# A two-layer diffusion step on one core: the first MLP's modulation sums and residual adds move from GpSimd and ScalarE to VectorE

## Chip, cores and metric

The kernel runs on one core of a Trainium2 chip. The metric is the device time of one launch in microseconds (us), the median of several runs. Engines: PE is TensorE (matrix products; its weight loads are listed as PEld), DVE is VectorE, ACT is ScalarE, POOL is GpSimd. SP only issues DMAs, in the order of its queue.

## The reference, cut to what matters

Two layers (one of differential attention, one of neighbourhood attention), each followed by a dense MLP, over 640 tokens (512 latent, 128 context) of width 1024. Every sub-layer has shift, scale and gate vectors that come from a conditioning vector. There are two conditions, `c` for the latent tokens and `c_ctx` for the context tokens, so each of the six vectors of a layer exists twice.

```python
def modulation(cond, w_ada_l, b_ada_l):
    m = (jax.nn.silu(cond) @ w_ada_l + b_ada_l)[:, None, :]
    return jnp.split(m, 6, axis=-1)

def mlp_residual(x, shift, scale, gate, g, w1, w2):
    h = rms_norm(x, g) * (1 + scale) + shift
    return x + gate * (jnp.square(jax.nn.relu(h @ w1)) @ w2)

for l in range(DEPTH):
    mp = modulation(cond_ctx, w_ada[l], b_ada[l])
    ms = modulation(c, w_ada[l], b_ada[l])
    ...
    yp = mlp_residual(yp, mp[3], mp[4], mp[5], norm_mlp_g[l], w_fc1[l], w_fc2[l])
    ys = mlp_residual(ys, ms[3], ms[4], ms[5], norm_mlp_g[l], w_fc1[l], w_fc2[l])
```

## The kernel before

All products are split into float32r parts: every operand is a high part (a ScalarE copy, L55) and a low part (a subtraction, L56, on VectorE here), and each product is three matmuls (hi·hi, hi·lo, lo·hi).

**The first MLP** runs from 473 to 932 us of the span, in four quarters q of 1024 hidden columns. In each, `fc1` loads three blocks of weights, makes eight column tiles `pz` of 48 matmuls each (L1076), and turns each into a tile `u`: ReLU and square on ScalarE, then the two parts. `fc2` then takes three blocks of columns (384, 256 and 384 wide) times five token tiles, in pairs (0, 1), (2, 3) and (4), 24 matmuls each (L160). `add_gated` closes each: VectorE multiplies the PSUM by the gate into `tmp` (L984), and then `tmp` is added to `x` (L985), on GpSimd in the first MLP and on VectorE in the second. The last block of q = 3 is a function of its own (`last_chunk`), with the add on VectorE already.

In the first block of a quarter the last two of the eight steps over the hidden columns are left to the end, for tile 0 and then for tile 1. In the built order PE's rest of tile 1 stands behind a wait for tile 0's `tmp`, since both lie in one PSUM tile. So VectorE's queue at that place can stop PE. I call it the boundary of a quarter.

**Beside it** `ada_fma` computes 14 half vectors of modulation without PE: the gate of layer 0's MLP and all six vectors of layer 1. A half vector (a job) is eight units: a DMA brings 128 rows of 512 columns (`fraw`, 256 KB, a ring of five buffers), and for both conditions the rows times a scalar per partition are added to `acc`. Condition 0 is one VectorE instruction (L439). Condition 1 is a ScalarE product into `ftmp` (two buffers, L441) and a GpSimd addition (L442). The first unit of a job writes instead of adding (L436 on VectorE, L437 on ScalarE). A finished job is summed over the partitions by PE: with eight transposes (L406) and a VectorE sum (L407) for shift and scale, with eight products by ones (L417) and a VectorE add (L418) for a gate. A gate goes to DRAM (L421); layer 0's is read back to all partitions (L453) and is wanted by the first `tmp`. 24 units are taken over the first fc1, the rest over the quarters that follow.

**What sets the order**: in this stretch a scheduler orders each engine's instructions from its own estimate of their times. Every engine, and SP's queue, then runs its list in order, and an instruction that waits holds back all behind it.

Of the kernel before, what the change touches and what calls it, by code (L numbers as in the profile page):

```python
# [7 lines left out]
F32 = mybir.dt.float32  # L8
F32R = mybir.dt.float32r
AF = mybir.ActivationFunctionType  # L10
ALU = mybir.AluOpType
# [4 lines left out]
P = 128  # L16
# [29 lines left out]
class Kernel:  # L46
# [333 lines left out]
                    nc.sync.dma_start(self.gate_d[l, vec // 3, :, c0 : c0 + 256], row)  # L380
            yield

    def ada_fma(self, jobs, pool, ahead, gate=None, share=False, wait=()):

        nc = self.nc
        units = [(job, kt) for job in jobs for kt in range(KT)]  # L390
        raws = []

        def load():
            (l, vec, h), kt = units[len(raws)]
            raw = pool.tile([P, 512], F32, tag="fraw", bufs=ahead + 1, name="fraw")
            nc.sync.dma_start(raw, self.I["w_ada"][l, kt * P : (kt + 1) * P, vec * D + h * 512 : vec * D + h * 512 + 512])
            raws.append(raw)

        def finish(l, vec, h, acc):
            c0 = vec * D + h * 512  # L400
            if vec % 3 < 2:
                pv = self.small.tile([P, 4, 2], F32, tag="pv", bufs=2, name="pv")
                for ci in range(2):
                    pt = self.psum_t()
                    for k in range(4):
                        nc.tensor.transpose(pt[:, k], acc[:, ci, k * P : (k + 1) * P], self.ident)  # L406
                    nc.vector.tensor_reduce(pv[:, :, ci], pt, AX.X, ALU.add)  # L407
                self.cols_out(l, vec, h * 4, 4, pv)
                return

            pb = self.psum_g(256)
            row = pool.tile([P, 512], F32, tag="ftmp", bufs=2, name="row")[:, 0:256]
            for j in range(4):
                cs = slice(j % 2 * 256, j % 2 * 256 + 256)
                src = self.I["b_ada"][l : l + 1, c0 + cs.start : c0 + cs.stop]
                nc.sync.dma_start(row[32 * j : 32 * j + 32], src.partition_broadcast(32))
                nc.tensor.matmul(pb[32 * j : 32 * j + 32], self.ones[:, 0:32], acc[:, j // 2, cs], start=True, stop=True)  # L417
            nc.vector.tensor_tensor(row, pb, row, ALU.add)  # L418
            for j in range(4):
                dst = self.gate_d[l, vec // 3, j // 2 : j // 2 + 1, h * 512 + j % 2 * 256 : h * 512 + j % 2 * 256 + 256]  # L420
                nc.sync.dma_start(dst, row[32 * j : 32 * j + 1])  # L421
            if l == 0 and h == 1:
                self.load_gate(0, gate)

        for _ in range(ahead):
            load()
        yield
        done = None
        for i, (job, kt) in enumerate(units):
            if i + ahead < len(units):  # L430
                load()
            raw = raws[i]
            s = [self.silu[:, ci, kt : kt + 1] for ci in range(2)]
            if kt == 0:
                acc = pool.tile([P, 2, 512], F32, tag="acc", bufs=2, name="acc")
                nc.vector.tensor_scalar(acc[:, 0], raw, s[0], None, ALU.mult)  # L436
                nc.scalar.activation(acc[:, 1], raw, AF.Identity, scale=s[1])  # L437
            else:
                nc.vector.scalar_tensor_tensor(acc[:, 0], raw, s[0], acc[:, 0], ALU.mult, ALU.add)  # L439
                tmp = pool.tile([P, 512], F32, tag="ftmp", bufs=2, name="ftmp")  # L440
                nc.scalar.activation(tmp, raw, AF.Identity, scale=s[1])  # L441
                (nc.vector if share and kt % 3 == 2 else nc.gpsimd).tensor_tensor(acc[:, 1], acc[:, 1], tmp, ALU.add)  # L442
            if done and kt == dict(wait).get(i // KT, 4):
                finish(*done)
            if kt == KT - 1:
                done = (*job, acc)
            yield
        finish(*done)
        yield

# [657 lines left out]
    def fc2(self, l, q, us, gate, fill, chunks=CHUNKS):  # L1108
        act = lambda kt, t: (us[kt][:, 0, t * P : (t + 1) * P], us[kt][:, 1, t * P : (t + 1) * P])
        for c0, n in chunks:  # L1110
            ww = self.load_block(self.I["w_fc2"][l], q * D, c0, n)

            for ts in ((0, 1), (2, 3), (4,)):
                if len(ts) == 2:
                    pair = self.psum.tile([P, 2, 512], F32, tag="s", bufs=self.PS, name="ps_g")
                    ps = [pair[:, i, :n] for i in range(2)]
                else:
                    ps = [self.psum_g(n)]
                late = KT - 2 if c0 == 0 and ts[0] == 0 else KT
                for i, t in enumerate(ts):  # L1120
                    for _ in self.product_steps(ps[i], act, t, ww, 0, late, last=late == KT):
                        pass
                for i, t in enumerate(ts):
                    if late < KT:
                        for _ in self.product_steps(ps[i], act, t, ww, late, KT, first=False):
                            pass
                    self.add_gated(self.x[t], ps[i], gate, t, c0, n, c0, None if l else self.nc.gpsimd)
                    if l and q == 3:
                        self.store(t, c0, n)
                    fill.go(n / D / NT / 2)  # L1130
# [226 lines left out]
```

## Time and profile before

| | us |
|---|---|
| median of 3 runs (1768.11 to 1772.25) | 1770.71 |
| the profiled execution | 1769.35 |
| its span | 1767.6 |
| PE busy in the span | 1696.0 (96%) |
| DVE busy | 1059.5 (60%) |
| ACT busy | 881.7 (50%) |
| POOL busy | 591.5 (33%) |

Matmuls overlap each other and their weight loads, so PE's mean duration of one is longer than its share of the time; a count over a stretch gives the pace. [...] The second MLP has the same matmuls as the first, without the modulation beside it.

### The profile page before, as it was taken

The numbers are of one execution on the slowest core, as the hardware profiler recorded it, in microseconds if no ns is written. First come the engines' busy times: TensorE is split into PE (matmuls) and PEld (weight loads), VectorE is DVE, ScalarE is ACT, GpSimd is POOL, SyncE is SP. The second block draws the span as 40 slices with busy tenths as digits, with TensorE's granted clock in tenths as the row PEclk, the third lists the DMA queues.
The fourth block names the chain that finished last, engine by engine and source line by source line (L and its number), as shares of the span: only waits on it lengthen the run. The fifth ranks groups of instructions, "written<-read, shape, count | busy, mean of one in ns | idle before, by whom it ended". The sixth has DMA issues, their size and how long they took to land.

```text
span 1767.6 us, 30599 instructions
## 1 busy us (share of the span) xinstructions
PE 1696.0 (96%) x11365; PEld 1617.8 (92%) x11365; DVE 1059.5 (60%) x2148; ACT 881.7 (50%) x2491; POOL 591.5 (33%) x630
## 2 busy tenths in 40 slices
PE   7899999988998999989999999999989999999999
PEld 4689999978898999989998999998889999999999
DVE  5568888865797667456746666667572433424323
ACT  4466777753663453533526777777354232142230
POOL 1333444234566436435326644553350000000000
PEclk9899999999999999999999999999999999999999
DMA  9862355321355444434422433333132222222221
GB/s 301 238 190 68 77 132 154 93 90 37 121 178 167 131 143 137 145 108 128 135 85 65 124 81 100 97 102 90 46 120 60 87 73 69 85 71 73 71 92 51
DMA packets 210435, 195.11 MB, mean 110 GB/s; under 512 B 39446, under 2 KB 194126, under 8 KB 210286
## 3 DMA queue, kind: packets, MB, share of 16 engines
q1 hardware_dynamic: 210286, 193.16, 37.2%
q8 instruction: 89, 1.46, 0.4%
q14 instruction: 60, 0.49, 0.1%
HBM read 182.96 MB, written 16.45 MB: 113 GB/s over the span
## 4 chain that ended last, share of the span: by engine, by line
PE 77%; ACT 7%; DVE 6%; POOL 3%; issue 3%; DMA 3%; SPq 1%; DVEq 0%; POOLq 0%; ACTq 0%
PE ps_g L160 43%; PE pz L1076 21%; PE ps_t L724 2%; PE ps_t L898 2%; PE ps_t L753 1%; PE ps_s L748 1%; PE ps_s L747 1%; PE ps_t L887 1%; DVE acc L439 1%; POOL acc L442 1%; ACT E L797 1%; POOL rs L132 1%; ACT sq L643 1%; ACT rawh L650 1%; ACT hf L480 1%
## 5 line engine op out<-in xcount | busy, mean ns | idle before, releaser
L160 PE MATMUL ps_g<-w,hT 128*128 128x384 f32 (+1 forms) x2544 | 541.5, 348 | 11.3 <-DVE tmp L984 4.8
L160 PE MATMUL ps_g<-w,u 128*128 128x384 f32 (+1 forms) x2880 | 455.0, 319 | 13.9 <-DVE tmp L984 12.7
L160 PEld LDWEIGHTS ps_g<-w,u 128*128 128x128 f32 x2880 | 448.0, 189 | 17.8 <-DVE tmp L984 12.7
L1076 PE MATMUL pz<-hT,w 128*128 128x320 f32 x3072 | 457.9, 310 | 5.6 <-ACT hT L55 2.5
L1076 PEld LDWEIGHTS pz<-hT,w 128*128 128x128 f32 x3072 | 451.1, 188 | 9.4 <-ACT hT L55 3.6
L160 PEld LDWEIGHTS ps_g<-w,hT 128*128 128x128 f32 x2544 | 426.4, 192 | 24.3 <-ACT hT L55 6.3
L55 ACT ACTIVATE w<-raw 128x1152 fp32r<-128x1152 f32 (+1 forms) x162 | 150.2, 955 | 218.3 <-PE ps_g L160 204.9
L56 DVE TENSOR_TENSOR w<-raw,w 128x1152 fp32r<-128x1152 f32 (+1 forms) x150 | 183.0, 1243 | 103.8 <-ACT w L55 103.6
L984 DVE TENSOR_TENSOR tmp<-ps_g,gate 128x384 f32<-128x384 f32 (+1 forms) x170 | 82.8, 505 | 223.2 <-PE ps_g L160 219.8
L442 POOL TENSOR_TENSOR acc<-acc,ftmp 128x512 f32<-128x512 f32 x98 | 164.5, 1679 | 131.5 <-ACT acc L437 103.7
L132 POOL TENSOR_TENSOR rs<-var,mhalf 128x4 f32<-128x4 f32 (+1 forms) x120 | 103.0, 861 | 233.6 <-DVE var L131 231.3
L121 POOL TENSOR_TENSOR w<-raw,w 128x256 fp32r<-128x256 f32 x184 | 142.9, 796 | 85.7 <-ACT w L117 84.6
L985 POOL TENSOR_TENSOR x<-x,tmp 128x384 f32<-128x384 f32 (+1 forms) x95 | 94.0, 1002 | 165.7 <-DVE tmp L984 165.0
L56 DVE TENSOR_TENSOR u<-relu,u 128x640 fp32r<-128x640 f32 x64 | 63.6, 994 | 117.6 <-ACT u L55 117.5
L441 ACT ACTIVATE ftmp<-fraw,silu 128x512 f32<-128x512 f32 x98 | 70.8, 723 | 118.4 <-POOL acc L442 96.0
L1101 ACT ACTIVATE relu<-pz 128x640 f32<-128x640 f32 x64 | 44.7, 699 | 169.4 <-PE pz L1076 169.4
L439 DVE SCALAR_TENSOR_TENSOR acc<-fraw,silu,acc 128x512 f32<-128x512 f32 x98 | 127.3, 1299 | 2.7 <-DMA fraw<-in_w_ada 0.4
L650 ACT ACTIVATE rawh<-ps_g,rs 128x64 f32<-128x64 f32 x304 | 71.0, 325 | 40.4 <-POOL rs L132 40.4
L748 PE MATMUL ps_s<-kT,qT 128*128 128x320 f32 (+3 forms) x256 | 76.1, 302 | 0.0
L747 PE MATMUL ps_s<-kT,qT 128*128 128x320 f32 (+3 forms) x256 | 75.8, 307 | 0.2 <-ACT E L797 0.2
L643 ACT ACTIVATE sq<-ps_g 128x64 f32<-128x64 f32 x304 | 68.3, 225 | 7.2
L872 DVE CUSTOM_DVE_ANT_0 ps_s<-ps_s,bias 128x384 f32<-128x384 f32 x64 | 36.2, 566 | 43.8 <-PE ps_s L748 31.8
(183 smaller groups left out, 2066.2 us busy)
## 6 DMA issues: line engine op xcount, KB each, us to landing
raw<-in_w_fc SPq DMA_DIRECT2D x64, 576.0 KB
fraw<-in_w_ada SPq DMA_DIRECT2D x112, 256.0 KB
raw<-in_w_fc SPq DMA_DIRECT2D x64, 384.0 KB
raw<-in_w_qkv_diff SPq DMA_DIRECT2D x24, 512.0 KB
fraw<-in_w_ada SPq DMA_DIRECT2D x24, 512.0 KB
raw<-in_w_qkv_na SPq DMA_DIRECT2D x24, 512.0 KB
bias<-ball SPq DMA_DIRECT2D x64, 128.0 KB
araw<-in_w_ada SPq DMA_DIRECT2D x8, 768.0 KB
```

The costliest lines, as they stand in the source:

```text
L55: self.nc.scalar.activation(hi, src, AF.Copy)
L56: (eng or self.nc.vector).tensor_tensor(lo, src, hi.bitcast(F32), ALU.subtract)
L121: self.nc.gpsimd.tensor_tensor(lo[:, ks], raws[i][:, ks], hi[:, ks].bitcast(F32), ALU.subtract)
L132: nc.gpsimd.tensor_tensor(out, v[:, :n], self.mhalf[:, :n], ALU.pow)
L160: self.nc.tensor.matmul(ps, a, b, start=first and kt == k0 and i == 0, stop=last and kt == k1 - 1 and i == 2)
L439: nc.vector.scalar_tensor_tensor(acc[:, 0], raw, s[0], acc[:, 0], ALU.mult, ALU.add)
L442: (nc.vector if share and kt % 3 == 2 else nc.gpsimd).tensor_tensor(acc[:, 1], acc[:, 1], tmp, ALU.add)
L650: nc.scalar.activation(raw[:, u // 2, u % 2], ps[:, u * 64 : u * 64 + 64], AF.Identity, scale=rs[:, u : u + 1])
L747: self.nc.tensor.matmul(out, q[:, 0, u], k, start=True, stop=False)
L748: self.nc.tensor.matmul(out, q[:, 1, u], k, start=False, stop=True)
L985: (eng or nc.vector).tensor_tensor(x[:, c0 : c0 + n], x[:, c0 : c0 + n], tmp, ALU.add)
L1076: nc.tensor.matmul(pz[:, s, 0:HALF], wp[:, cs], self.hT[:, b, kt, s * HALF : (s + 1) * HALF], start=first and kt == 0, stop=last and kt == ...
```

## The change

For condition 1 the ScalarE product and the GpSimd addition are replaced by a second VectorE instruction of the form that condition 0 has. `add_gated` in `fc2` adds to `x` on VectorE in both layers. The gates' `row` gets a pair of buffers of its own, since the buffers that it shared with `ftmp` go.

```diff
-            row = pool.tile([P, 512], F32, tag="ftmp", bufs=2, name="row")[:, 0:256]
+            row = pool.tile([P, 256], F32, tag="frow", bufs=2, name="row")
...
                 nc.vector.tensor_scalar(acc[:, 0], raw, s[0], None, ALU.mult)
                 nc.scalar.activation(acc[:, 1], raw, AF.Identity, scale=s[1])
             else:
-                nc.vector.scalar_tensor_tensor(acc[:, 0], raw, s[0], acc[:, 0], ALU.mult, ALU.add)
-                tmp = pool.tile([P, 512], F32, tag="ftmp", bufs=2, name="ftmp")
-                nc.scalar.activation(tmp, raw, AF.Identity, scale=s[1])
-                (nc.vector if share and kt % 3 == 2 else nc.gpsimd).tensor_tensor(acc[:, 1], acc[:, 1], tmp, ALU.add)
+                for ci in range(2):
+                    nc.vector.scalar_tensor_tensor(acc[:, ci], raw, s[ci], acc[:, ci], ALU.mult, ALU.add)
...
-                    self.add_gated(self.x[t], ps[i], gate, t, c0, n, c0, None if l else self.nc.gpsimd)
+                    self.add_gated(self.x[t], ps[i], gate, t, c0, n, c0)
```

PE's order stays as it was, and so does the order of everything before and after the first MLP. On VectorE, ScalarE, GpSimd and SP the first MLP is ordered anew. Two places on VectorE follow. In the names, `u` and `w` are the low parts of hidden tiles and of weights, and `gate_6385` is the gate for the latent tokens.

VectorE ahead of the boundary of q = 0, from the add that closes the second half of layer 0's gate to the first `tmp`; before:

```order
L418 TENSOR_TENSOR row<-ps_g,row 128x256
L436 TENSOR_SCALAR acc<-fraw,silu 128x512
L439 SCALAR_TENSOR_TENSOR acc<-fraw,silu,acc 128x512 x2
L56 TENSOR_TENSOR w<-raw,w 128x3x256
L56 TENSOR_TENSOR u<-relu,u 128x640
L439 SCALAR_TENSOR_TENSOR acc<-fraw,silu,acc 128x512
L56 TENSOR_TENSOR w<-raw,w 128x3x256
L56 TENSOR_TENSOR w<-raw,w 128x2x256
L439 SCALAR_TENSOR_TENSOR acc<-fraw,silu,acc 128x512 x2
L984 TENSOR_TENSOR tmp<-ps_g,gate_6385 128x384
```

The same place of the changed kernel (its L440 is L439 of before, L982 and L983 are L984 and L985):

```order
L418 TENSOR_TENSOR row<-ps_g,row 128x256
L436 TENSOR_SCALAR acc<-fraw,silu 128x512
L440 SCALAR_TENSOR_TENSOR acc<-fraw,silu,acc 128x512 x4
L56 TENSOR_TENSOR u<-relu,u 128x640
L440 SCALAR_TENSOR_TENSOR acc<-fraw,silu,acc 128x512 x2
L56 TENSOR_TENSOR w<-raw,w 128x3x256 x2
L56 TENSOR_TENSOR w<-raw,w 128x2x256
L982 TENSOR_TENSOR tmp<-ps_g,gate_6385 128x384
L440 SCALAR_TENSOR_TENSOR acc<-fraw,silu,acc 128x512
L983 TENSOR_TENSOR x<-x,tmp 128x384
```

Six instead of five accumulations stand between the row and `tmp`, and the last `u` has four of them ahead of it. From the start of the MLP to this `tmp` there are 48 accumulations instead of 26.

VectorE ahead of the boundary of q = 2, from the first accumulation behind a job's two sums (L407) to `tmp`; before:

```order
L439 SCALAR_TENSOR_TENSOR acc<-fraw,silu,acc 128x512
L333 TENSOR_TENSOR ab_84<-ab_84,cols 128x4
L56 TENSOR_TENSOR w<-raw,w 128x3x256
L56 TENSOR_TENSOR u<-relu,u 128x640
L439 SCALAR_TENSOR_TENSOR acc<-fraw,silu,acc 128x512
L56 TENSOR_TENSOR w<-raw,w 128x3x256
L56 TENSOR_TENSOR w<-raw,w 128x2x256
L439 SCALAR_TENSOR_TENSOR acc<-fraw,silu,acc 128x512 x2
L984 TENSOR_TENSOR tmp<-ps_g,gate_6385 128x384
```

and of the changed kernel:

```order
L440 SCALAR_TENSOR_TENSOR acc<-fraw,silu,acc 128x512
L333 TENSOR_TENSOR ab_84<-ab_84,cols 128x4
L440 SCALAR_TENSOR_TENSOR acc<-fraw,silu,acc 128x512
L56 TENSOR_TENSOR u<-relu,u 128x640
L440 SCALAR_TENSOR_TENSOR acc<-fraw,silu,acc 128x512 x2
L56 TENSOR_TENSOR w<-raw,w 128x3x256 x2
L56 TENSOR_TENSOR w<-raw,w 128x2x256
L440 SCALAR_TENSOR_TENSOR acc<-fraw,silu,acc 128x512
L982 TENSOR_TENSOR tmp<-ps_g,gate_6385 128x384
```

Five accumulations instead of four stand ahead of `tmp`, and all three parts of the weights now follow `u`.

## Rows read from the trace of the kernel before

**Rows 1.** Windows: us, busy us (instructions) of PE, PEld, DVE, ACT, POOL; clock.

```profile
473.00:932.00 459.00, 442.69 (x2945) 436.26 (x2945) 304.05 (x313) 200.33 (x276) 222.21 (x157) 0.99 0.45 137
...
1323.00:1747.00 424.00, 423.84 (x2834) 423.28 (x2833) 147.10 (x210) 124.89 (x163) 1.29 (x1) 1.00 0.24 74
```

**Rows 2.** What PE waited for in the first MLP: us in total, times, longest.

```profile
PE ps_g L160 <- DVE tmp L984: 12.7, 3, 6.0
PE pz L1076 <- DVE w L56: 1.4, 2, 1.1
PE ps_g L160 <- DVE u L56: 0.9, 1, 0.9
PE pz L1076 <- ACT relu L1101: 0.8, 1, 0.8
```

**Rows 3.** Timeline of PE: start us, us, line, output<-inputs, count, [idle before <-releaser].

```profile
473.26 28.13 PE L1076 MATMUL pz<-hT,w 128*128 128x320 f32 x190 [0.17 <-DVE hT L56]
...
542.51 17.74 PE L160 MATMUL ps_g<-w,u 128*128 128x384 f32 x99 [5.71 <-DVE tmp L984]
...
781.87 25.86 PE L160 MATMUL ps_g<-w,u 128*128 128x384 f32 x169 [6.04 <-DVE tmp L984]
...
1323.34 49.25 PE L1076 MATMUL pz<-hT,w 128*128 128x320 f32 x334 [0.16 <-DVE hT L56]
```

**Rows 4.** Timeline of DVE, same columns.

```profile
489.31 11.11 DVE L439 SCALAR_TENSOR_TENSOR acc<-fraw,silu,acc 128x512 f32<-128x512 f32 x7
...
540.46 1.53 DVE L439 SCALAR_TENSOR_TENSOR acc<-fraw,silu,acc 128x512 f32<-128x512 f32 x2
541.90 0.55 DVE L984 TENSOR_TENSOR tmp<-ps_g,gate 128x384 f32<-128x384 f32 x1
...
767.11 1.29 DVE L407 TENSOR_REDUCE pv<-ps_t 128x4 f32<-128x512 f32 x2 [4.37 <-PE ps_t L406]
...
931.95 0.56 DVE L984 TENSOR_TENSOR tmp<-ps_g,gate 128x384 f32<-128x384 f32 x1 [3.38 <-PE ps_g L160]
...
1746.89 0.56 DVE L984 TENSOR_TENSOR tmp<-ps_g,gate 128x384 f32<-128x384 f32 x1 [3.27 <-PE ps_g L160]
```

**Rows 5.** Chain that ended last: start us, us, line, count.

```profile
600.32 0.87 PE ps_t L406 x8
...
696.32 0.57 PE ps_g L417 x8
```

**Rows 6.** Windows of 1 us, columns as in rows 1.

```profile
540.00:541.00 1.00, 0.00 (x0) 0.00 (x0) 1.00 (x2) 0.72 (x1) 0.00 (x0) 0.50 0.00 0
...
544.00:545.00 1.00, 1.00 (x5) 1.00 (x4) 0.16 (x1) 0.00 (x0) 1.00 (x1) 0.50 0.94 202
```

**Rows 7.** Groups of the first MLP: count, busy us, mean ns, idle before <-releasers.

```profile
L442 POOL TENSOR_TENSOR acc<-acc,ftmp 128x512 f32<-128x512 f32 x98 | 164.5, 1679 | 131.5 <-ACT acc L437 103.7 <-ACT ftmp L441 23.4
L439 DVE SCALAR_TENSOR_TENSOR acc<-fraw,silu,acc 128x512 f32<-128x512 f32 x98 | 127.3, 1299 | 2.7 <-DMA fraw<-in_w_ada 0.4 <-DVE acc L439 0.2
L441 ACT ACTIVATE ftmp<-fraw,silu 128x512 f32<-128x512 f32 x98 | 70.8, 723 | 118.4 <-POOL acc L442 96.0 <-DMA fraw<-in_w_ada 21.0 <-POOL x L985 1.1
...
L985 POOL TENSOR_TENSOR x<-x,tmp 128x384 f32<-128x384 f32 (+1 forms) x55 | 55.0, 1017 | 104.6 <-DVE tmp L984 104.6
```

**Rows 8.** The same view by form, second MLP, DVE, where GpSimd does nothing.

```profile
L56 DVE TENSOR_TENSOR w<-raw,w 128x1152 fp32r<-128x1152 f32 x30 | 40.1, 1357 | 49.6 <-ACT w L55 49.4
L56 DVE TENSOR_TENSOR w<-raw,w 128x768 fp32r<-128x768 f32 x29 | 27.4, 954 | 23.2 <-ACT w L55 23.2
L56 DVE TENSOR_TENSOR u<-relu,u 128x640 fp32r<-128x640 f32 x32 | 26.3, 823 | 92.6 <-ACT u L55 92.6
L985 DVE TENSOR_TENSOR x<-x,tmp 128x384 f32<-128x384 f32 x40 | 21.3, 554 | 0.7
```

**Rows 9.** Timelines of PE and SP's queue: the gate's sums, its read-back.

```profile
526.18 0.64 PE L417 MATMUL ps_g<-acc,ones 128*32 128x256 f32 x8
...
531.39 0.83 SPq L453 DMA_DIRECT2D gate<-gate_d  x2
```

More of the change, by code (lines that the diff above doesn't have):

```diff
@@ L381, in ada_cols, with ada_fma @@
             yield
-    def ada_fma(self, jobs, pool, ahead, gate=None, share=False, wait=()):
+    def ada_fma(self, jobs, pool, ahead, gate=None, wait=()):
         nc = self.nc
```

## The prediction, made before the changed kernel ran

> **What bounds the kernel now.** I read the windows first. In the first MLP PE is busy 442.69 of 459 us, in the second 423.84 of 424 [rows 1]. The matmuls are the same, so the second MLP shows what the first could be. From the first unbroken run of fc1 to the first `tmp` of the last block the first takes 931.95 - 473.26 = 458.69 us and the second 1746.89 - 1323.34 = 423.55 [rows 3, 4], 35.14 more. The modulation's own work on PE accounts for eight jobs of 0.87 and six of 0.57 us [rows 5], 10.4. So 24.7 us are lost to other things, and that is the most that this change can give back: PE's order stays, and the products for L406 and L417 stay too.
>
> Then the list of PE's waits says where: 12.7 us for `tmp`, 1.4 for low parts of weights, 0.9 for a `u`, 0.8 for a ReLU [rows 2], 15.8 together. Two of the three waits for `tmp` carry nearly all: 5.71 us ahead of 542.51 (boundary of q = 0) and 6.04 ahead of 781.87 (q = 2) [rows 3]. [...]
>
> In both long stops PE waits for VectorE, and VectorE is not waiting for anything: it is late with its own list. What makes it late is GpSimd. Seven accumulations (L439) beside a running GpSimd took 11.11 us, 1.59 each; two of them at 540.46, when GpSimd stood idle (its busy time in that us is 0.00 [rows 6]), took 541.90 - 540.46 = 1.44 us, 0.72 each [rows 4]. The mean over all 98 is 1.30, and GpSimd's own addition takes 1.68 [rows 7].
>
> **The change part by part.**
>
> *Condition 1 on VectorE.* A unit cost VectorE up to 1.59 us and GpSimd 1.68 at the same time; now it costs VectorE 2 x 0.72 = 1.44 and nobody else. Each engine's list is in order, so what counts is VectorE's list up to the `tmp` that PE waits for. For q = 0 that is 48 accumulations x 0.72 = 34.6 us; eight `u` x 0.82 = 6.6; nine parts of weights, four of 1.36 and five of at most 0.95, 10.2 [rows 8]; six short instructions (L436, L418) at 0.72 as an upper bound, 4.3. Sum 55.7. PE stopped at 542.51 - 5.71 = 536.80; without its earlier waits of 1.4 + 0.8 + 0.9 this becomes 533.7, which leaves 60.4 us from 473.3. The list fits, but it must not stand and wait for long, and it does so once: the add of the second gate half (L418) needs the products that PE makes at the end of fc1, at 526.18 before [rows 9], 524.0 without the waits for weights and ReLU. Behind them (0.64) come L418 and L436 (0.72 each at most), six accumulations (4.3), the last `u` (0.82) and three parts of weights (2.85), 9.4 in all: `tmp` starts at 534.0 and ends at 534.6, so PE stands 0.9 us instead of 5.71.
>
> For q = 2 the same count starts at the two sums at 767.11 (1.29) [rows 4]: the short ones behind them 1.1 (an estimate: 0.72 for L436, 0.1 for each of four instructions on 128x4), five accumulations 3.6, `u` 0.82, weights 2.85: `tmp` starts at 776.8 and ends at 777.3. PE stops at 781.87 - 6.04 = 775.83, so 1.5 us are left of 6.04. The third wait for `tmp`, under 1 us, and those for weights, `u` and ReLU go: VectorE and ScalarE reach these earlier.
>
> [...]
>
> *ScalarE's 98 products of 0.72 go*, with the 96.0 us that they waited for GpSimd [rows 7]. ScalarE is in order, and its ReLU, square and high parts stood behind those waits. It bounds nothing afterwards: 200.33 - 70.8 = 130 us of work in the stage [rows 1, 7]. I count this at nothing beside the waits above.
>
> *The addition to `x` on VectorE*: 55 instructions [rows 7] at 0.55 or less [rows 8], at most 30 us more. Each stands behind its `tmp`, which frees the PSUM, so PE meets it only if the next `tmp` is late. In fc2 a pair of tiles is 48 matmuls at 0.15 on average (169 in 25.86 us [rows 3]), over 7 us, while two `tmp` and two adds take 2.2 and five accumulations beside them 3.6. Cost on the path: nothing. If that cover were gone, it would be 0.55 per block's pair.
>
> *The whole of VectorE*: 304.05 us in the stage now [rows 1]; the accumulations go from 127.3 to 196 x 0.72 = 141, the adds bring 30, and the rest shrinks without GpSimd beside it; I expect 310 to 335 of some 438. It stays off the bound outside the two places above.
>
> *The queues.* On SP the loads of weights now stand behind other `fraw` loads, and a `fraw` waits for VectorE alone instead of ScalarE and VectorE. ScalarE waited 21.0 us for `fraw` [rows 7], because the ring came free late; I count nothing and keep it as a rival. The read-back of the gate (L453) was issued 531.39 - 526.18 = 5.2 us behind the products [rows 9] and had landed by 540, when the DMA engines were at rest [rows 6].
>
> *Sum.* 24.7 lost; 0.9 + 1.5 remain at the two boundaries, and I keep 1.3 for small waits that I can't place. 24.7 - 3.7 = 21.0. The profiled execution took 1769.35 and becomes 1748.4; it lies 1.36 below the median of 1770.71, which becomes 1749.7. After the MLP PE runs on with what it finds ready, so the time is kept to the end. I forecast 1750.
>
> **The rivals.**
>
> *The gate comes back late.* Only the first `tmp` needs it. If L453 again starts 5.2 us behind the products (524.0 + 5.2 = 529.2) and takes all of the 540 - 531.39 = 8.6 that are the upper bound, `tmp` can't end before 538.4 and PE stands 4.7 instead of 0.9: 1754. For it: VectorE's L418 now has a free engine in front, so the path is the DMAs' own. Against: the bound is loose, since the DMA engines moved five other loads in that time.
>
> *`fraw` becomes the bound.* VectorE consumes 256 KB in 1.44 us, faster than before, and a late load now stops the same list that holds `u`, `w` and `tmp`. If half of the 21.0 us that ScalarE waited pass to places where PE feels them, 1749.7 + 10.5 = 1760.
>
> *The accumulation is slow by itself, not for GpSimd's sake* (slower). Then 48 of them at the mean of 1.30 [rows 7] add 48 x 0.58 = 27.8 us to the list of q = 0, of which 4.7 of slack are taken off: 23.1 more at that boundary, and 5 x 0.58 = 2.9 at q = 2. That is 26 above 1749.7, 1776. It turns from gain to loss where the 21 are used up, at (21 + 4.7) / (48 + 5) = 0.48 above 0.72, an accumulation of 1.2 us. Against it stand the two of 0.72. [...]
>
> *No change.* Accumulations of 1.1 to 1.2 us, or time that a later stage takes back. I see no stage behind it that PE reaches and finds waiting for something timed otherwise. That the change doesn't do what it says is out: GpSimd's list has neither addition any more.
>
> **How the numbers follow.** The forecast 0.64; the gate 0.08; `fraw` 0.12; no change 0.07; slower 0.09. A measurement of this kernel tells 0.2%, 3.5 us, from no change. Faster is 0.64 + 0.08 + 0.12 = 0.84, same 0.07, slower 0.09. The range begins where all 24.7 are regained (1746), 1 us lower for the spread of runs, and reaches over the `fraw` rival with as much: 1745 to 1761. It leaves out no change and slower, 0.16.
>
> **What will show it.** The accumulations' mean falls to 0.75 us or less, with 196 of them; GpSimd has no addition in the first MLP. PE's waits for `tmp` in the first MLP fall from 12.7 to about 2.4, those for weights, `u` and ReLU under 1, and the granted clock stays at 1.00. VectorE is busy 310 to 335 us there. The stretch of 458.69 us becomes some 438. I am wrong if the mean stays above 1 us, if VectorE stands waiting for `fraw` for more than 5 us, or if the stretch shortens and the span doesn't.

## The result, and the profile after

The changed kernel takes 1748.09 us (median of 4 runs, 1746.34 to 1748.59); the kernel before, measured beside it, 1770.04. The ratio is 0.9874, 95% interval 0.9857 to 0.9891: 1.3% faster, where 1750 was forecast. The profiled execution took 1746.34 with a span of 1744.5, 23.1 us less than before.

The windows of the first MLP, columns as in [rows 1]; the last three are TensorE's granted clock as a share of full speed, the DMA engines' mean busy share and GB/s:

```profile
473.00:932.00 459.00, 457.48 (x3072) 452.97 (x3073) 308.67 (x499) 149.18 (x206) 16.98 (x20) 1.00 0.45 140
```

PE is busy 457.48 of 459 us instead of 442.69, and GpSimd has 17 us of work where it had 222. The same window now holds the first matmuls of what follows, for the stage ends earlier. What PE waited for, from 473 to 915 us (us in total, times, longest), is one line, where [rows 2] had four with 15.8 us:

```profile
PE pz L1074 <- DVE hT L56: 0.2, 1, 0.2
```

PE's timeline over the two boundaries that carried the long stops of [rows 3]:

```profile
473.08 28.13 PE L1074 MATMUL pz<-hT,w 128*128 128x320 f32 x190 [0.16 <-DVE hT L56]
...
523.02 0.64 PE L417 MATMUL ps_g<-acc,ones 128*32 128x256 f32 x8
523.59 26.93 PE L160 MATMUL ps_g<-w,u 128*128 128x384 f32 x168
...
753.83 32.36 PE L160 MATMUL ps_g<-w,u 128*128 128x384 f32 x216
```

Both runs of fc2 (L160) are unbroken from their first matmul over the boundary. VectorE's timeline at the places of [rows 4]:

```profile
483.16 4.73 DVE L440 SCALAR_TENSOR_TENSOR acc<-fraw,silu,acc 128x512 f32<-128x512 f32 x7
...
523.73 0.42 DVE L418 TENSOR_TENSOR row<-ps_g,row 128x256 f32<-128x256 f32 x1 [4.53 <-PE ps_g L417]
524.07 0.48 DVE L436 TENSOR_SCALAR acc<-fraw,silu 128x512 f32<-128x512 f32 x1
524.49 2.74 DVE L440 SCALAR_TENSOR_TENSOR acc<-fraw,silu,acc 128x512 f32<-128x512 f32 x4
527.15 0.81 DVE L56 TENSOR_TENSOR u<-relu,u 128x640 fp32r<-128x640 f32 x1
527.88 1.41 DVE L440 SCALAR_TENSOR_TENSOR acc<-fraw,silu,acc 128x512 f32<-128x512 f32 x2
529.21 2.42 DVE L56 TENSOR_TENSOR w<-raw,w 128x768 fp32r<-128x768 f32 x3
531.55 0.55 DVE L982 TENSOR_TENSOR tmp<-ps_g,gate 128x384 f32<-128x384 f32 x1
...
753.67 1.29 DVE L407 TENSOR_REDUCE pv<-ps_t 128x4 f32<-128x512 f32 x2 [4.38 <-PE ps_t L406]
...
761.96 0.55 DVE L982 TENSOR_TENSOR tmp<-ps_g,gate 128x384 f32<-128x384 f32 x1
...
909.80 0.56 DVE L982 TENSOR_TENSOR tmp<-ps_g,gate 128x384 f32<-128x384 f32 x1 [3.27 <-PE ps_g L160]
```

Seven accumulations in a row take 4.73 us, where seven took 11.11. The first `tmp` of q = 0 starts at 531.55, 8.0 us behind the first matmul of fc2, and PE does not stop. The stretch that the prediction measured, from the first unbroken run of fc1 to the first `tmp` of the last block, is 909.80 - 473.08 = 436.72 us, where it was 458.69: 21.97 of the 23.1 us are here. The groups of VectorE in the first MLP, columns as in [rows 7]:

```profile
L440 DVE SCALAR_TENSOR_TENSOR acc<-fraw,silu,acc 128x512 f32<-128x512 f32 x196 | 135.1, 746 | 1.1 <-DMA fraw<-in_w_ada 1.1
L56 DVE TENSOR_TENSOR w<-raw,w 128x1152 fp32r<-128x1152 f32 (+2 forms) x66 | 70.8, 1106 | 25.4 <-ACT w L55 25.2
L983 DVE TENSOR_TENSOR x<-x,tmp 128x384 f32<-128x384 f32 (+1 forms) x60 | 30.6, 533 | 0.5
L982 DVE TENSOR_TENSOR tmp<-ps_g,gate 128x384 f32<-128x384 f32 (+1 forms) x60 | 29.1, 508 | 60.8 <-PE ps_g L160 60.8
L56 DVE TENSOR_TENSOR u<-relu,u 128x640 fp32r<-128x640 f32 x32 | 26.3, 821 | 28.6 <-ACT u L55 28.5
```

There are twice as many accumulations, 196, and they cost 135.1 us, where 98 cost 127.3 [rows 7]. VectorE waits for `fraw` 1.1 us in all. That it waits 60.8 us for PE to finish a PSUM tile is by itself no sign that it is ahead of PE, for before it waited 73.1 us; that PE waits for none of its `tmp`, `u` and `w` any more is.

### The profile page after: what moved, and what is told of

Same layout as the page of the kernel before. It is cut to its first block, busy times and chain, and to the rows that moved or that the text cites. A ratio compares the mean times of both kernels' runs of the same rounds, so it can differ in the third digit from the quotient of the medians.

```text
span 1744.5 us, 30268 instructions
## 1 busy us (share of the span) xinstructions
PE 1687.0 (97%) x11365; PEld 1610.6 (92%) x11365; DVE 1047.6 (60%) x2301; ACT 815.6 (47%) x2393; POOL 372.7 (21%) x477
## 4 chain that ended last, share of the span: by engine, by line
PE 81%; ACT 7%; DVE 4%; DMA 3%; POOL 3%; issue 2%; SPq 1%; POOLq 0%; DVEq 0%; ACTq 0%
PE ps_g L160 43%; PE pz L1074 25%; PE ps_t L722 2%; PE ps_t L896 2%; PE ps_t L751 1%; PE ps_s L746 1%; PE ps_s L745 1%; PE ps_t L885 1%; ACT E L795 1%; POOL rs L132 1%; ACT hf L478 1%; ACT sq L641 1%; ACT rawh L648 1%; DVE hT L56 1%; DVE x L983 1%
## 5 line engine op out<-in xcount | busy, mean ns | idle before, releaser
L160 PE MATMUL ps_g<-w,hT 128*128 128x384 f32 (+1 forms) x2544 | 540.4, 347 | 12.4 <-ACT hT L55 5.5
L160 PE MATMUL ps_g<-w,u 128*128 128x384 f32 (+1 forms) x2880 | 449.8, 317 | 0.0
L160 PEld LDWEIGHTS ps_g<-w,hT 128*128 128x128 f32 x2544 | 425.2, 192 | 25.7 <-ACT hT L55 7.7
L160 PEld LDWEIGHTS ps_g<-w,u 128*128 128x128 f32 x2880 | 444.3, 188 | 2.2 <-issue 1.2
L56 DVE TENSOR_TENSOR w<-raw,w 128x1152 fp32r<-128x1152 f32 (+1 forms) x150 | 164.0, 1120 | 101.1 <-ACT w L55 100.7
L982 DVE TENSOR_TENSOR tmp<-ps_g,gate 128x384 f32<-128x384 f32 (+1 forms) x170 | 82.8, 505 | 208.0 <-PE ps_g L160 207.9
L440 DVE SCALAR_TENSOR_TENSOR acc<-fraw,silu,acc 128x512 f32<-128x512 f32 x196 | 135.1, 746 | 1.1 <-DMA fraw<-in_w_ada 1.1
L56 DVE TENSOR_TENSOR u<-relu,u 128x640 fp32r<-128x640 f32 x64 | 52.6, 822 | 121.2 <-ACT u L55 121.0
L983 DVE TENSOR_TENSOR x<-x,tmp 128x384 f32<-128x384 f32 (+1 forms) x130 | 72.0, 576 | 1.7
L641 ACT ACTIVATION_READ_ACCUMULATOR sq<-ps_g 128x1 f32 x304 | 60.4, 199 | 0.0
L795 ACT ACTIVATE E<-ps_s,nm 128x640 f32<-128x640 f32 (+1 forms) x80 | 57.7, 724 | 2.6 <-DVE nm L793 2.1
## 6 DMA issues: line engine op xcount, KB each, us to landing
bias<-ball SPq DMA_DIRECT2D x64, 128.0 KB
```

What stands on the lines that cost most here:

```text
L56: (eng or self.nc.vector).tensor_tensor(lo, src, hi.bitcast(F32), ALU.subtract)
L160: self.nc.tensor.matmul(ps, a, b, start=first and kt == k0 and i == 0, stop=last and kt == k1 - 1 and i == 2)
L440: nc.vector.scalar_tensor_tensor(acc[:, ci], raw, s[ci], acc[:, ci], ALU.mult, ALU.add)
L641: nc.scalar.activation(sq, ps[:, u * 64 : u * 64 + 64], AF.Square, accum_out=ss[:, u : u + 1])
L983: (eng or nc.vector).tensor_tensor(x[:, c0 : c0 + n], x[:, c0 : c0 + n], tmp, ALU.add)
```

## The experiments

The theory: VectorE's instructions are slow only while GpSimd works beside them, this makes VectorE late at the places where PE needs it, and nothing else in the change matters. The rivals: the additions to `x` are what counts; the ScalarE product and its waits are; the new order on VectorE is; VectorE had simply too much to do. The kernel before ran beside each group of kernels, on one chip per group, so the ratios are what compares. The stretch is the one defined above, from the profiled execution; PE's waits are those inside it, without the 0.2 us for `hT` that every kernel has at its start (before has 0.3 for ReLU beside the 15.8 of [rows 2]).

| kernel | us | ratio to before [95%] | stretch | PE's waits in it |
|---|---|---|---|---|
| before | 1770.04 | 1 | 458.69 | 16.1 |
| changed | 1748.09 | 0.9874 [0.9857, 0.9891] | 436.72 | 0 |
| e1 accumulations only | 1746.92 | 0.9896 [0.9881, 0.9911] | 436.70 | 0 |
| e2 additions to `x` only | 1770.36 | 1.0032 [1.0019, 1.0045] | 460.47 | 18.0 |
| e3 ScalarE product kept | 1744.22 | 0.9883 [0.9868, 0.9897] | 436.98 | 0 |
| e4 GpSimd adds beside | 1768.28 | 1.0013 [1.0003, 1.0023] | 458.36 | 15.4 |
| e5 half as many of them | 1758.89 | 0.9942 [0.9926, 0.9958] | 447.72 | 5.7 |
| e9 GpSimd fills beside | 1747.79 | 0.9886 [0.9869, 0.9902] | 436.72 | 0 |
| e6 third sum on VectorE | 1753.88 | 0.9918 [0.9901, 0.9934] | 443.53 | 4.5 |
| e7 out_proj's additions too | 1750.73 | 0.9899 [0.9883, 0.9916] | 436.72 | 0 |
| e8 those of layer 0 alone | 1748.09 | 0.9886 [0.9871, 0.9902] | 436.72 | 0 |
| changed, beside e5 to e7 | 1747.19 | 0.9881 [0.9866, 0.9895] | 436.71 | 0 |
| changed, beside e8 and e3 | 1746.49 | 0.9876 [0.9856, 0.9895] | 436.71 | 0 |
| e3, beside e8 | 1747.08 | 0.9875 [0.9857, 0.9893] | 436.59 | 0 |

In the group of e1 to e4 the kernel before took 1765.70, 4.3 us less than in the result, so times there are lower all round: e1's and e3's fall below the ranges that were expected for them, and the ratios and the stretch are what tells.

### One half of the change at a time (e1, e2)

e1 is the changed kernel with the additions to `x` left on GpSimd; e2 is the kernel before with only those moved:

```diff
 e1, against the changed kernel
-                    self.add_gated(self.x[t], ps[i], gate, t, c0, n, c0)
+                    self.add_gated(self.x[t], ps[i], gate, t, c0, n, c0, None if l else self.nc.gpsimd)
 e2, against the kernel before
-                    self.add_gated(self.x[t], ps[i], gate, t, c0, n, c0, None if l else self.nc.gpsimd)
+                    self.add_gated(self.x[t], ps[i], gate, t, c0, n, c0)
```

> Half of the change: both accumulations on VectorE, the additions to x stay on GpSimd. Contention theory (VectorE's accumulation takes 0.72 us alone and 1.59 beside a running GpSimd, and that alone made it late at two boundaries): the 55 additions of about 1 us fall into fc2, behind the boundaries, so nearly all of the gain is there: 1748 to 1752, accumulations' mean 0.75 to 0.85, PE's waits for tmp under 3 us. If the additions to x carried a good part of the gain: 1756 or more.

> The other half: the additions to x on VectorE, condition 1 still a ScalarE product and a GpSimd addition. Contention theory: GpSimd's additions to acc stand beside VectorE ahead of both boundaries as before: 1767 to 1773, accumulations' mean about 1.3, two long waits for tmp. If the additions to x carried the gain: 1760 or less.

e1 has the whole gain: its stretch is 436.70, as in the changed kernel. GpSimd is still there for 65 us, and its additions (1.19 us in the mean, 1.02 before) and the accumulations (0.796, 0.746 in the changed kernel) slow each other a little, but not where PE feels it (the groups of e1):

```profile
L440 DVE SCALAR_TENSOR_TENSOR acc<-fraw,silu,acc 128x512 f32<-128x512 f32 x196 | 144.8, 796 | 1.3 <-DMA fraw<-in_w_ada 1.3
L983 POOL TENSOR_TENSOR x<-x,tmp 128x384 f32<-128x384 f32 (+1 forms) x55 | 64.7, 1190 | 368.0 <-DVE tmp L982 367.4 <-DVE ab L330 0.6
```

e2 gains nothing and is 0.3% slower. PE's timeline of e2 has both boundaries, with longer stops than the 5.71 and 6.04 of [rows 3]:

```profile
542.79 20.41 PE L160 MATMUL ps_g<-w,u 128*128 128x384 f32 x120 [7.61 <-DVE tmp L984]
...
782.17 25.73 PE L160 MATMUL ps_g<-w,u 128*128 128x384 f32 x169 [6.92 <-DVE tmp L984]
```

So the gain is the modulation's sums, and the additions to `x` are worth nothing beside them; alone they give VectorE more to do while its accumulations stay slow (1.27 us in the mean, 1.30 before).

### The ScalarE product (e3)

e3 keeps ScalarE's product for condition 1 and only moves its addition to VectorE:

```diff
-                for ci in range(2):
-                    nc.vector.scalar_tensor_tensor(acc[:, ci], raw, s[ci], acc[:, ci], ALU.mult, ALU.add)
+                nc.vector.scalar_tensor_tensor(acc[:, 0], raw, s[0], acc[:, 0], ALU.mult, ALU.add)
+                tmp = pool.tile([P, 512], F32, tag="ftmp", bufs=2, name="ftmp")
+                nc.scalar.activation(tmp, raw, AF.Identity, scale=s[1])
+                nc.vector.tensor_tensor(acc[:, 1], acc[:, 1], tmp, ALU.add)
```

> No GpSimd in the first MLP, but condition 1 keeps its ScalarE product into ftmp; the addition of it is VectorE's. Contention theory: VectorE pays 0.72 for each of the two, as in the changed kernel: 1748 to 1753. ScalarE theory (its 98 products and its waits held up ReLU and high parts, and that was what PE lost): ScalarE now waits for VectorE's additions in place of GpSimd's, so half of the gain or more is gone: 1758 to 1770, with waits of PE for ReLU, u and weights of 3 us or more.

Its groups in the first MLP:

```profile
L439 DVE SCALAR_TENSOR_TENSOR acc<-fraw,silu,acc 128x512 f32<-128x512 f32 x98 | 72.9, 744 | 1.0 <-DMA fraw<-in_w_ada 0.7
...
L441 ACT ACTIVATE ftmp<-fraw,silu 128x512 f32<-128x512 f32 x98 | 69.9, 719 | 68.7 <-DVE acc L442 58.2 <-DMA fraw<-in_w_ada 5.3 <-issue 3.2
L442 DVE TENSOR_TENSOR acc<-acc,ftmp 128x512 f32<-128x512 f32 x98 | 66.9, 683 | 1.3 <-ACT ftmp L441 0.7
```

ScalarE still makes its products and still waits ahead of them, now mostly for VectorE (68.7 us, where it was 118.4), and PE waits for nothing: the gain is whole. So ScalarE's 70.8 us had no part in the loss, and waits of 68.7 us cost nothing. It ran a second time beside the changed kernel, since 1744.22 looked lower than that:

> The kernel of e3 (ScalarE's product kept, its addition on VectorE) once more, on one chip with the changed kernel. By e3 the product costs nothing, for it lies beside VectorE's own work: within 1.5 us of the changed kernel. If the removal of ScalarE's 70 us was worth something, it is slower by more than that; if a plain addition (66 us in 98) is better than the accumulation that it stands for (135 us in 196), it is faster: 1743 to 1745 beside 1747.

1747.08 beside 1746.49: they are the same.

### GpSimd beside the changed kernel (e4, e5)

e4 is the changed kernel in which GpSimd adds every slice of the modulation's weights to a tile that nothing reads. PE, VectorE, ScalarE and SP keep the changed kernel's orders. e5 does it on every second slice (`if kt % 2`).

```diff
+        own = pool.tile([P, 512], F32, name="own")
+        nc.gpsimd.memset(own, 0.0)
...
                     nc.vector.scalar_tensor_tensor(acc[:, ci], raw, s[ci], acc[:, ci], ALU.mult, ALU.add)
+                nc.gpsimd.tensor_tensor(own, own, raw, ALU.add)
```

> The changed kernel, with a GpSimd addition of the old size (128x512) per unit beside it, into a tile of its own that nobody reads; the lists of PE, VectorE, ScalarE and SP are the changed kernel's. Contention theory: the accumulations' mean goes to 1.2 to 1.5 us, VectorE's list of 48 ahead of the first boundary grows by 23 to 37 us, of which some 7 are slack: 1765 to 1790, slower than or like the kernel before. Order theory (the gain comes from the new order of VectorE's and SP's lists) and ScalarE theory: 1747 to 1751.

> The changed kernel with half of the extra work of e4: on every second slice of the modulation weights GpSimd adds the slice to a tile of its own that nothing reads, 49 additions where e4 had 98. If the price is overlap with GpSimd, VectorE's accumulations lie between the two: a mean of about 0.90 us (halfway from 0.746 to 1.055), some 85 us of GpSimd in the stage, and a time between 1748 and 1768: 1750 to 1760. It needs not be halfway, since what the order has to spare is used up first: nearer to 1750 if VectorE's list has several us to spare at the borders of q, nearer to 1760 if it has none. If instead any GpSimd work beside this order upsets it whatever its amount, it is 1765 to 1770 as in e4.

e4 gives the whole gain back: stretch 458.36, ratio 1.0013. That rules out the new order by itself as the cause of the gain, for in the traces of both kernels PE, VectorE and ScalarE run the same instructions in the same order. The list of PE's waits in e4:

```profile
PE pz L1077 <- DVE w L56: 7.8, 1, 7.8
PE ps_g L160 <- DVE u L56: 5.0, 2, 4.3
PE ps_g L160 <- DVE tmp L985: 2.6, 2, 1.9
```

and the groups of e4:

```profile
L442 DVE SCALAR_TENSOR_TENSOR acc<-fraw,silu,acc 128x512 f32<-128x512 f32 x196 | 196.4, 1055 | 0.2 <-DMA fraw<-in_w_ada 0.2
L443 POOL TENSOR_TENSOR own<-own,fraw 128x512 f32<-128x512 f32 x98 | 170.1, 1736 | 241.4 <-DMA fraw<-in_w_ada 238.2
```

The accumulations wait for `fraw` only 0.2 us, so it isn't that GpSimd, as one more reader, holds the ring; they are longer themselves. Their mean of 1.055 is less than the 1.2 to 1.5 that I had expected, and yet all is given back. e5 lies between: mean 0.949, and 0.9942 is 46% of the way from 0.9881 (the changed kernel beside it) to e4's 1.0013. One accumulation of e5 and the GpSimd addition that it ran into, VectorE first:

```profile
494.40 1.79 DVE L442 SCALAR_TENSOR_TENSOR acc<-fraw,silu,acc 128x512 f32<-128x512 f32 x1
```

```profile
493.83 1.80 POOL L444 TENSOR_TENSOR own<-own,fraw 128x512 f32<-128x512 f32 x1 [1.24 <-DMA fraw<-in_w_ada]
```

It takes 1.79 us instead of 0.74, and ends 0.56 us behind GpSimd's.

### GpSimd busy, but reading nothing (e9)

e9 is e4 with three fills of the same tile in place of the addition:

```diff
+                for _ in range(3):
+                    nc.gpsimd.memset(own, 0.0)
```

> The changed kernel with GpSimd busy on something that reads nothing: three fills of its own 128x512 tile with zero for every unit of the modulation, 294 fills where e4 had 98 additions. They wait for nothing and so run in one piece from about 473 us on, some 147 us at the 0.525 us that one such fill took in e5, over the whole of q = 0 with its wait places. PE, VectorE and ScalarE have the orders of the changed kernel. If it is a running GpSimd as such that slows VectorE, the accumulations ahead of some 620 us take about 1.6 us, as in the kernel before, and the stops of e4 at 508 and 545 us return: 1760 to 1770. If it is the reading of SBUF by both engines, nothing slows: a mean of 0.75 us, `u` at 0.82, no waits of PE in the stage, 1745 to 1749. The traces so far speak for the second: `tmp`, with one of its two inputs in PSUM, took 0.554 us for 128x384 both before and after, and an addition on 128x4 with both inputs in SBUF (L333) took 0.98 us in the mean before and 0.16 after.

The windows of e9, from 480 to 600 us, which hold the boundary of q = 0, columns as in [rows 1]:

```profile
480.00:600.00 120.00, 120.00 (x805) 118.78 (x805) 97.23 (x156) 38.00 (x50) 108.29 (x204) 1.00 0.56 179
```

and its groups:

```profile
L442 DVE SCALAR_TENSOR_TENSOR acc<-fraw,silu,acc 128x512 f32<-128x512 f32 x196 | 134.9, 743 | 1.1 <-DMA fraw<-in_w_ada 1.1
```

GpSimd is busy 108.29 of 120 us, PE 120.00 of 120, and the accumulations have 0.743 us. The stretch is that of the changed kernel to the hundredth. The fills run from 475 to 648 us, so they cover the boundary of q = 0 alone; the 98 accumulations in that time take 0.733 to 0.753 us each. So a GpSimd that was busy with writing alone did these no harm (0.743 us); one that also read SBUF did (1.055 in e4). An accumulation reads two tiles there.

### More work for VectorE alone (e6)

e6 is the changed kernel with a third accumulation for every slice, into a tile that nothing reads. The scheduler puts the list of VectorE in another order for it.

```diff
+                own = pool.tile([P, 512], F32, tag="own", bufs=1, name="own")
+                nc.vector.tensor_scalar(own, raw, s[0], None, ALU.mult)
...
+                nc.vector.scalar_tensor_tensor(own, raw, s[0], own, ALU.mult, ALU.add)
```

> The changed kernel with a third accumulation on VectorE for every slice, into a tile that nothing reads: 98 instructions of the same form more, no GpSimd. It adds 98 x 0.67 = 66 us to VectorE's busy time in the stage (309 to some 375, about what e4 shows, 384). If VectorE has no room at the borders of q, where the modulation's 3 x 10 or so accumulations stand ahead of the gated products in its list, the matmuls wait there for tmp again: some 24 accumulations x 0.67 = 16 us more by the first border, less 7 to 10 us to spare, a stop of 6 to 9 us and about as much at the second: 1758 to 1766. If only overlap with GpSimd costs time and VectorE has room in its total (375 of 437 us), it stays at 1747 to 1750, with a mean of 0.74 and no waits of the matmuls. In both, the mean of an accumulation stays under 0.80 us, since GpSimd is idle.

VectorE is busy 374.36 us from 473 to 932, about what it is in e4 (384.33), and the time is 1753.88: 6.7 us more than the changed kernel beside it, where e4 gives back 21.6 by the stretch. The accumulations stay at 0.743, and none of the two boundaries stops PE. The one stop is earlier, in fc1 of q = 0, for parts of the weights. PE's timeline and the windows of 1 us around it:

```profile
502.35 0.85 PE L1077 MATMUL pz<-hT,w 128*128 128x320 f32 x4
507.75 22.84 PE L1077 MATMUL pz<-hT,w 128*128 128x320 f32 x140 [4.55 <-DVE w L56]
```

```profile
504.00:505.00 1.00, 0.00 (x0) 0.00 (x0) 1.00 (x2) 0.85 (x2) 0.00 (x0) 1.00 0.46 139
506.00:507.00 1.00, 0.00 (x0) 0.00 (x0) 1.00 (x2) 0.00 (x0) 0.00 (x0) 0.50 0.00 0
...
508.00:509.00 1.00, 1.00 (x5) 1.00 (x6) 1.00 (x2) 0.00 (x0) 0.00 (x0) 0.50 0.58 155
...
512.00:513.00 1.00, 1.00 (x8) 1.00 (x7) 1.00 (x2) 0.26 (x1) 0.00 (x0) 0.84 1.03 379
```

So both readings of mine missed: VectorE has not room for anything that fits its total, and it doesn't fail at the boundaries by 6 to 9 us each. The place where its list fails first is the weights of fc1. The stop of 4.55 us lengthened the stretch by 6.8: the granted clock falls to 0.50 while PE stands and stays there until 512, for some 4 us of matmuls. The 144 matmuls of the two lines above take 0.85 + 22.84 = 23.69 us, where 144 from 501.71 on take 21.39 in the changed kernel: these are the other 2.3 us.

### Taking it further (e7, e8)

e7 moves out_proj's additions to `x` to VectorE too; e8 does it in layer 0 alone.

```diff
-        self.add_gated(self.x[t], ps, gate, t, c0, n, 0, self.nc.gpsimd)
+        self.add_gated(self.x[t], ps, gate, t, c0, n, 0)
```

> The changed kernel, and the additions to x in out_proj moved from GpSimd to VectorE as well (40 additions, 39 us of GpSimd at 0.98 us each). By what e1 and e2 showed, additions alone are worth little: nothing in out_proj is bound by GpSimd (63 us of idle time ahead of these additions are waits for tmp). Expected within 3 us of the changed kernel, 1745 to 1751; up to 40 x 0.4 = 16 us of VectorE's time are freed by products that no longer meet GpSimd, and 40 x 0.55 = 22 us of it are newly taken. Slower than 1751 only if VectorE's list is what the matmuls wait for in out_proj.

> The changed kernel itself, beside the three others on the same chip, so that they are compared with it and not only with the kernel before: 1743 to 1749, 0.987 of the kernel before.

> The changed kernel, with the additions to x in out_proj on VectorE in the first layer alone (20 of the 40). In e7 the first MLP's first matmul came at 459.5 us, 2 to 2.6 us ahead of both traces of the changed kernel (461.6 and 462.1), and the stretch from the first MLP's end to the second MLP's first matmul took 386.1 us, where the changed kernel's two traces have 379.0 and 380.8: a gain in the first layer's out_proj and a loss in the second's. If that reading holds, this keeps the gain without the loss: 1744 to 1746 beside the changed kernel's 1747. Against it stands that kernels with an untouched out_proj have their first matmul of the MLP at 459.9 to 462.2 us, so that the 2 us can be scatter: then it is the time of the changed kernel within 1.5 us.

> The changed kernel, for the comparison of the other two on the same chip: 1745 to 1749, 0.987 to 0.989 of the kernel before.

e7 took 1750.73 beside the changed kernel's 1747.19, with overlapping intervals; e8 1748.09 beside 1746.49. Neither is better. The 2 us that I had read into e7's first layer were scatter: e8's first matmul of the MLP came at 462.57. The loss in its second layer lies outside of the scatter: from the first MLP's end to the second MLP's first matmul e7 takes 386.1 us, e8 381.8, and the seven other traces without waits 378.3 to 380.8. In e7's one trace PE waits 4.0 us there for low parts of `hT` from VectorE, 0.8 in the changed kernel; why they are late wasn't followed up. I found no version that beats the changed kernel.

## Why the prediction was right, point by point

*What bounds the kernel.* Right. The two long stops and all the small ones are gone, and the stretch is 436.72 where some 438 was forecast. Four readings support that VectorE was late because of GpSimd: it comes with the sums alone (e1), is given back by GpSimd's reads alone in an unchanged order (e4), by half with half of them (e5), and not at all by a GpSimd that reads nothing (e9).

*What can be regained.* The floor was put at 423.55 + 10.4 = 433.95. It is 436.7: the nine traces of the table in which PE waits for nothing lie between 436.59 and 436.98. So the 24.7 us that could be had were in truth 22, and all of them came. That all of it goes with the stops was an estimate: 15.8 of it were waits [rows 2], and of the other 8.9 [rows 6] show only that the granted clock was 0.50 at and behind one stop. The stops cost 5.9 us beside the 16.1 of waiting; 3.6 of these are PE working at a granted clock of 0.50 to 0.88 behind the two stops, estimated from windows of 1 us as in [rows 6] (PE's busy time in each, times what its clock lacks to 1.00). The other 2.8 us, 436.7 less 433.95, lie between the two MLPs without any wait. In the changed kernel's trace fc2 of q = 0, from 523.59 to 580.92, takes 57.33 us, and the same in its second MLP 55.30, with one job of 0.80 (550.36 to 551.16) to account for 2.03. Nearly all of the other 1.2, and over the whole stretch some 2.4 of the 2.8, is the pace of fc2's matmuls, from one start to the next: in the first MLP more of them have 176.7 ns (128x384) or 117.8 (128x256), in the second more have 173.3 or 113.3, at a granted clock of 1.00 in both. The first 120 of fc2 take 21.31 us from 523.59 on, and 20.90 from 1349.38 on in the second MLP. What sets this pace stays open.

*The accumulations at 0.72.* Right in size: 0.746 by their records, and 0.67 from one start to the next in a row (524.49 to 527.15 for four).

*The list up to `tmp`.* The step that was mis-sized. For q = 0 I had put 9.4 us between the gate's products and `tmp`, and it took 531.55 - 523.73 = 7.82. In its terms: the short ones 0.76 instead of 1.44 (taken at an upper bound), six accumulations 3.99 instead of 4.3, `u` 0.73 instead of 0.82, the parts of weights 2.34 instead of 2.85. The products were 1.0 us earlier as well (523.02 instead of 524.0). `tmp` ended at 532.1 instead of 534.6, ahead of the 533.7 at which I had PE stop, so the 0.9 us of stop never came. For q = 2 I had 9.7 from the sums to `tmp`, and it took 761.96 - 753.67 = 8.29: the short ones 0.68 for 1.1, five accumulations 3.32 for 3.6, `u` and the weights as above. It ends 8.84 behind the sums where PE was forecast to stop at 8.72, and the stop of 1.5 is none. The cause is the same in both: for `u` and the weights I summed durations, where starts are closer together than durations, for the short ones I took bounds and a guess of 0.1 for each on 128x4 (0.16 by their records, 0.07 from start to start), and the 0.72 of an accumulation was the distance of one pair, where it is 0.67 here. Why a duration is the longer of the two, 0.746 against 0.67 for an accumulation, no trace here shows. It is close all the same. PE had stopped behind 48 matmuls of fc2 in q = 0 and 47 in q = 2, which PE now reaches at 532.18 and 762.23, and `tmp` ends at 532.10 and 762.51. That no wait is left at all is partly luck, and why the second `tmp` doesn't stop PE for a moment the records don't show.

*The sum.* The 3.7 us that I left as a residue were not waits: 0.9 and 1.5 are zero, and for the 1.3 stand the 2.8 that the floor was too low by. 21.0 was forecast and the stretch gave 21.97, so two errors of opposite sign, a residue 3.7 too high and a floor 2.8 too low, nearly cancel: that the forecast came so near is partly luck. The remaining 1.1 of the span's 23.1 is within the scatter: what lies behind the stretch takes 834.7 to 836.7 us in three traces of the changed kernel and 835.7 before.

*ScalarE's products and the additions to `x` at nothing.* Right, by e3 and e1. That the additions cost something while the sums are left on GpSimd (e2, stretch 1.8 us longer) I had not considered.

*The whole of VectorE.* Put too high: 310 to 335 us were forecast, and in the stretch it is busy 292.23. I had given no number for what shrinks without GpSimd beside it; the `u` and the weights alone went from 128.0 to 98.4 us.

*The rivals.* The gate's read-back was issued 525.89 - 523.02 = 2.9 us behind the products instead of 5.2, and `tmp` never waited for it. SP's timeline:

```profile
525.89 0.84 SPq L451 DMA_DIRECT2D gate<-gate_d  x2
```

`fraw` held VectorE 1.1 us. An accumulation that is slow by itself is out with 0.746. I had put the turn from gain to loss at a mean of 1.2 us; with e4's 1.055 the gain is already gone. What was missing there is that the others suffer with it: `u` and the weights on the same list slow down beside GpSimd too (a `u` takes 1.05 us in the mean in e4, 0.82 in the changed kernel), and I had moved the accumulations alone.

## What to carry to other kernels

When an engine is late without waiting for anything, compare what one of its instructions takes with another engine busy and at rest: the same VectorE accumulation took 0.67 us alone and 1.59 beside GpSimd additions, so two on VectorE were cheaper than one on each. Before part of a sum goes to GpSimd, look whether both engines would read SBUF for it; GpSimd fills cost the accumulations nothing here (0.743 us beside them in e9, 0.746 in the changed kernel), and VectorE's products out of PSUM were not slowed (0.554 before and after). And size a list by the distance of starts (0.67 for an accumulation), not by the sum of durations (0.746). A short wait of TensorE cost more than it lasted: 16.1 us of waits cost 22.0 before, 15.4 cost 21.6 in e4, 4.5 cost 6.8 in e6, and the 5.7 of e5, in four waits of at most 2.5, cost 11.0. Nearly all of what came on top in e4 to e6 lies in the runs of matmuls that the stops break: by PE's timelines these took 6.3 us longer than the same matmuls of the changed kernel in e4, 5.2 in e5 and 2.3 in e6. PE at a granted clock below 1.00 accounts for an estimated 3.6 of 5.9 before and for all of it in e6, by windows of 1 us.

## What the runs showed of the hardware that I had not expected

Beside GpSimd the length of a VectorE instruction said little of its size. VectorE's timeline before the change has the same small product on 128x4 (L333, which the expectation of e9 called an addition) twice within 1 us:

```profile
768.78 0.16 DVE L333 TENSOR_TENSOR ab<-ab,cols 128x4 f32<-128x4 f32 x1
...
769.59 1.27 DVE L333 TENSOR_TENSOR ab<-ab,cols 128x4 f32<-128x4 f32 x1
```

and GpSimd's at that place:

```profile
769.43 5.29 POOL L442 TENSOR_TENSOR acc<-acc,ftmp 128x512 f32<-128x512 f32 x3 [20.17 <-ACT acc L437]
```

With GpSimd idle it takes 0.16 us, and 1.27 when it starts just behind a GpSimd addition: the first of the three additions ends at 770.84 and L333 at 770.86, as if it had waited for that addition to end. Another instruction was not touched at all. The product by the gate, with one input in PSUM, has the same length in the groups of before

```profile
L984 DVE TENSOR_TENSOR tmp<-ps_g,gate 128x384 f32<-128x384 f32 x36 | 19.2, 554 | 61.9 <-PE ps_g L160 58.7 <-issue 3.2
```

and of the changed kernel:

```profile
L982 DVE TENSOR_TENSOR tmp<-ps_g,gate 128x384 f32<-128x384 f32 x40 | 21.4, 554 | 48.3 <-PE ps_g L160 48.3
```

Two runs set such instructions apart by what is read. The accumulation, with two tiles of SBUF as inputs, took 1.055 us in the mean in e4, where GpSimd reads SBUF too, and 0.743 in e9, where it only writes; `tmp`, with one of its inputs in PSUM, took 0.549 in e4 and 0.553 in e9. An instruction with a single tile as input was not free of GpSimd either: the first write of a job, a product of one tile by a scalar, took 0.72 us in the mean before and 0.48 in the changed kernel, and in e9, where GpSimd only writes, 0.48 to 0.93 in the seven cases beside the fills and 0.48 in each of the seven behind them. Two of those beside the fills:

```profile
475.06 0.93 DVE L438 TENSOR_SCALAR acc<-fraw,silu 128x512 f32<-128x512 f32 x1 [1.56 <-DMA fraw<-in_w_ada]
...
503.42 0.48 DVE L438 TENSOR_SCALAR acc<-fraw,silu 128x512 f32<-128x512 f32 x1
```

GpSimd pays as well: its additions to `x` took 1.02 us in the mean before and 1.19 in e1, beside a VectorE with twice the accumulations. And where PE waited for nothing the chip repeated itself closely: the stretch came out at 436.70 to 436.72 us in seven of nine traces, while what lies behind it varied by 2 us between the three traces of the changed kernel alone.
